# Attention weights of first halves turned by TensorE instead of by transfer, in a two-layer decoder trunk

## The chip, the cores and the metric

The kernel runs on one core of one Trainium2 chip. The metric is device time in microseconds (us) of one execution. The kernel before takes 1116.9 us, the median of three runs from 1115.07 to 1117.86.

## The reference

Two pre-norm residual layers work on 1024 positions of width 1024, and a last RMSNorm closes. Layer 0 is an RG-LRU: an input product, a causal convolution, two block-diagonal gates, a linear recurrence, an output product. Layer 1 is attention with a forget gate, 16 heads of 64. Cut to what matters here:

```python
u = h @ w_in                       # q, k, v, gate, f_logit
cum = cumsum(log_sigmoid(f_logit + b_f))
logits = einsum("bqhd,bkhd->bhqk", q, k) / 8
logits = logits + cum_q[..., None] - cum_k[:, None]
logits = where(kpos <= qpos, logits, -1e30)
o = einsum("bhqk,bkhd->bqhd", softmax(logits), v)
x = x + (o * silu(gate)) @ w_out
return rms_norm(x, final_g)
```

All inputs and outputs are float32.

## The kernel before

TensorE does nearly all products three times, in a format of its own for float32 (hi x hi, hi x lo, lo x hi), where hi is a rounded copy (`to_hi`, a cast) and lo the rest (`to_lo`, a subtraction). Layer 0 fills the first 447 us or so and the change doesn't touch it. Attention runs from about 484 us on, head by head, and is what this document is about.

**A head.** The 1024 queries of a head are two halves `c` of 512, and each half has four rows `i` of 128 queries. Row `i` sees keys 0 to (i+1) x 128. `maxima(hd, c)` makes the rows of one half, from the longest down: TensorE multiplies into a PSUM tile `S`; DVE adds the mask and finds the maximum (L773); ACT takes exp (L778) into a tile `p` (or `pp`, a tile that holds two rows). After the rows of the second half the sums are turned into factors: their transpose goes to `rc`, by DMA to `recd`, and comes back as `recb`, spread over partitions (`fetch_sums`). `weigh(hd, c)` then multiplies the weights with the values into `O`. For that the weights must stand with keys on the partitions, so they have to be turned. There are two ways:

- by TensorE: 128x128 transposes (L61) into a PSUM tile `pt`, out of which ACT writes `ph` (hi) and DVE `pl` (lo). `pt` has two slots in PSUM and shares them with `S`, so every tile of the one kind waits for the slot that an earlier one of either kind leaves;
- by transfer (`by_dma`): for the two longest rows of a half, DVE turns 32x32 blocks (`turn_row`, L733), one DMA writes them to DRAM (`turnd`, L738 or L740), and four DMAs read them back into `pp` in the order wanted (L745). `ph` and `pl` are then read from `pp`. The remaining blocks of that half go through TensorE.

**Sections.** Head `hd` has two sections. The first runs `weigh(hd, 0)` beside `maxima(hd, 1)`: rows 7, 6, 5, 4 of S. The second runs `weigh(hd, 1)` beside `maxima(hd + 1, 0)`: rows 3, 2, 1, 0 of the next head. Each is driven by a string, where `1` is the next step of `maxima`, `0` the next step of `weigh`, and `.` one fill step: six 128x512 matmuls, about 1.39 us of TensorE, of the projections of later heads (`kq_units`, `g_units`) or, in the last heads, of the output product. The strings are `ORDER` for heads 0 to 11 and `LAST` for heads 12 to 15. A `side` generator gives one step per fill step: stores of y, sums, scaling, weights.

**The other parts that the change touches.** `scale(hd)` multiplies the gate `sg` by `recb` on GpSimd (POOL), and `gated(hd, c)` multiplies `yo` by it, also on POOL; `put_away` splits y and stores it; `settle` calls `fetch_sums`, `scale` and `gated(hd, 0)` in the second section. After heads 3, 7 and 11 come the values of the next four heads: `value_weights` loads and splits their weights in the second section, and `values` makes 192 matmuls of 128x256 (tile `vps`). `late` loads and splits, in head 14, the part of the output weights that is used last (L1092); its raw tiles `wf` come from the same ring of three buffers as those of `split_out` (L108), which feed the output product that fills TensorE at that time. SP's queue issues all DMAs, one after the other.

Of the kernel before, what the change touches and what calls it, by code (L numbers as in the profile page):

```python
# [11 lines left out]
F32 = mybir.dt.float32  # L12
# [5 lines left out]
P = 128  # L18
SEQ = 1024
HALF = 512  # L20
# [3 lines left out]
HD = 64  # L24
EPS = 1e-6
GROUP = 2
ORDER = "1.0.1.10.1..0", "10.1.0.10.1.0.0"
LAST = "1..0.1..10..1..0", "10..1.0..10..1.0..0"
NEG = -1e30
PSUM = bass.MemoryType.PSUM  # L30
# [8 lines left out]
def trunk(ctx: ExitStack, tc: tile.TileContext, xt, w0, wg, wo0, pc, gn, gf, w1, wv, wf, bf, wo1, out):  # L39
# [11 lines left out]
    wpool = ctx.enter_context(pool("w", 4))  # L51
# [450 lines left out]
    with ExitStack() as l1:  # L502
# [24 lines left out]
        def value_weights(g, parts):  # L527

            waiting = []
            for k in range(0, KT + 2, 2):  # L530
                if k < KT:
                    wt = wpool.tile([P, 2, 256], F32, tag="wf", name="wf", bufs=3)
                    nc.sync.dma_start(wt, wv[g, :, k : k + 2])
                    waiting.append(wt)
                if k:
                    own = wpool if k <= 4 else vwpool
                    hi = own.tile([P, 2, 256], F32R, tag="wh", name="wh")
                    lo = own.tile([P, 2, 256], F32R, tag="wl", name="wl")
                    with tc.issue_after(seen[0].ins):
                        to_hi(hi, waiting[0], nc.scalar)  # L540
                    with tc.issue_after(masked[0].ins):
                        to_lo(lo, waiting.pop(0), hi, nc.vector)
                    parts += [(hi[:, i], lo[:, i]) for i in range(2)]
                yield

        def values(g, parts):

# [171 lines left out]
            return two_rows[c][:, r * size : r * size + n]  # L719

        def by_dma(hd, c):
            return 0 < 2 * hd + c < 27

        written, turns = [None], {}

# [82 lines left out]
        def scale(hd, cs=slice(0, SEQ)):  # L808
            rows = slice((hd % 2) * HD, (hd % 2 + 1) * HD)
            for b in range(cs.start, cs.stop, HALF):  # L810
                part = slice(b, b + HALF)
                sg = sgs[hd // 2][rows, part]
                nc.gpsimd.tensor_tensor(sg, sg, recs[hd // 2][rows, part], ALU.mult)  # L813
# [93 lines left out]
        def gated(hd, c, sub=slice(0, HALF)):  # L907

            if hd % 2 == 0:
                return  # L910
            pair = hd // 2
            yo = yos[pair, c][:, sub]
            nc.gpsimd.tensor_tensor(
                yo, yo, sgs[pair][:, c * HALF + sub.start : c * HALF + sub.stop], ALU.mult
            )
            if hd == 15:
                split_y(c, pair, yo, sub)

        def put_away(hd, c):
            if hd % 2 == 0 or hd > 12:  # L920
                return
            pair = hd // 2
            yo = yos[pair, c]
            yh = at.tile([P, HALF], F32R, tag="xp", name="yh", bufs=2)
            with tc.issue_after(seen[0].ins):
                to_hi(yh, yo, nc.scalar)
            with tc.issue_after(masked[0].ins):
                to_lo(yo.bitcast(F32R), yo, yh, nc.vector)
            for part, y in enumerate((f32(yh), yo)):
                nc.sync.dma_start(y1d[c, pair, part], y)  # L930

        def settle(hd):
            yield
            yield
            with tc.issue_after(written[0].ins):
                fetch_sums(hd)
            yield
            scale(hd)
            gated(hd, 0)

        def put_later(hd):
            for c in range(2):
                yield
                yield
                put_away(hd, c)

        def beside(*gens):
            for _ in itertools.zip_longest(*gens):
                yield
# [135 lines left out]
        def late():  # L1085

            for half in range(2):
                wh, wl = (kqpool.tile([P, 8, P], F32R, tag=f"qk{p}{half}", name=f"wo{p}") for p in "hl")
                for b in range(2):
                    wt = wpool.tile([P, 4, P], F32, tag="wf", name="wf", bufs=3)  # L1090
                    for d in range(2):
                        nc.sync.dma_start(wt[:, 2 * d : 2 * d + 2], wo1[half * 4 + b * 2 + d, :, 6:8])  # L1092
                    sl = slice(4 * b, 4 * b + 4)

                    with tc.issue_after(seen[0].ins):
                        to_hi(wh[:, sl], wt, nc.scalar)
                    to_lo(wl[:, sl], wt, wh[:, sl], nc.vector)
                    yield
                late_w.append((wh, wl))
# [16 lines left out]
        for hd in range(HEADS):  # L1116
# [18 lines left out]
            elif pair < 6:  # L1135
                fill = chain(kq_units(pair + 1, ((0, (1,)),)), late_q(hd + 1), g_units(pair + 1))
            first, second = LAST if hd > 11 else ORDER
            side = put_later(hd - 1) if hd else iter(())
            run(first, weigh(hd, 0), maxima(hd, 1), fill=fill, side=side)
            drain(side)  # L1140
            if hd == HEADS - 1:
# [4 lines left out]
                scale(hd)  # L1146
            side = late() if hd == 14 else settle(hd)
            if hd % 4 == 3 and hd < 12:

                parts = []  # L1150
                side = beside(side, value_weights(hd // 4 + 1, parts))
            run(second, weigh(hd, 1), maxima(hd + 1, 0), fill=fill, side=side)
            drain(side)
            gated(hd, 1)
            if hd == 13:
                with tc.issue_after(seen[0].ins):
                    split_y(0, 6, yos[6, 0])
# [90 lines left out]
```

## Time and profile before

| | |
|---|---|
| median of three runs | 1116.9 us |
| lowest and highest | 1115.07 and 1117.86 us |
| profiled execution | 1114.79 us |
| its span | 1113.0 us |
| mean granted TensorE clock | 0.995 |
| TensorE busy | 1088.5 us of the span |

The span goes from the first to the last instruction of the profiled execution; the 1.8 us between it and the execution's own time lie around the program. The profiled execution is 2.1 us shorter than the median. "Busy" is the time in which an engine executes; a TensorE matmul's end is modelled, so its idle times are read from the start of one matmul to the start of the next. A row of the timeline gives start, duration, engine, line, operation and tile; in brackets stands the idle time before it and who ended it. In the windows view a row has the stretch, its length, the busy time of PE (matmuls), PEld (weight loads), DVE, ACT and POOL with their instructions, the granted clock (1.00 is full), the share of the DMA engines and GB/s.

### The profile page before, as it was taken

To read this page: it belongs to the slowest core of one execution; us is meant where nothing else is said; L and a number is where in the kernel's file an instruction comes from. 1 tells how busy PE (TensorE), PEld (TensorE's weight loads), DVE (VectorE), ACT (ScalarE), POOL (GpSimd) and SP (SyncE) were. 2 spreads that over 40 slices of the span, in tenths; PEclk is the share of its full clock that TensorE was granted. 3 is DMA by queue.
4 is the path that set the end of the run, shared out by engine and by line. 5 is a ranking of instruction groups with operands and counts; after the bars stand their busy time and mean duration, and the time that the engine had idled before them with its cause. 6 is when DMAs were issued, how large, how long until landed. Compare 5 with 4: busy or idle time off the path is not lost.

```text
span 1113.0 us, 15892 instructions
## 1 busy us (share of the span) xinstructions
PE 1088.5 (98%) x5645; PEld 921.1 (83%) x5645; DVE 792.1 (71%) x1280; ACT 579.9 (52%) x1037; POOL 171.8 (15%) x120
## 2 busy tenths in 40 slices
PE   9999999999999999999999999999999999998997
PEld 7787888888888888987888888788888898887886
DVE  8888755876569787757887478874788757666445
ACT  8487345355454665545555355553556535434335
POOL 2312212111121201420121101111012110110010
PEclk9999999999999999999999999999999999999999
DMA  6111111111112113445767357674477845785344
GB/s 220 62 53 42 52 53 48 48 54 45 43 48 71 48 65 116 130 124 162 199 192 195 118 161 193 200 198 123 150 189 213 198 126 166 248 266 174 109 147 189
DMA packets 100919, 145.81 MB, mean 131 GB/s; under 512 B 25348, under 2 KB 53636, under 8 KB 100840
## 3 DMA queue, kind: packets, MB, share of 16 engines
q1 hardware_dynamic: 100840, 144.80, 43.6%
q8 instruction: 44, 0.72, 0.3%
q14 instruction: 35, 0.29, 0.1%
HBM read 83.48 MB, written 36.11 MB: 107 GB/s over the span
## 4 chain that ended last, share of the span: by engine, by line
PE 76%; DVE 7%; DMA 6%; issue 5%; ACT 4%; SPq 1%; POOL 1%; ACTq 0%; DVEq 0%; POOLq 0%
PE gps L57 26%; PE ops L57 16%; PE ups L57 10%; PE vps L57 7%; PE S L57 5%; PE O L57 4%; PE gate L57 3%; PE turn L57 2%; PE pt L61 2%; DVE pl L98 2%; ACT pp L778 1%; DMA T<-qkl 1%; DVE S L773 1%; DMA U<-qkh 1%; DMA turnd<-turn 1%
## 5 line engine op out<-in xcount | busy, mean ns | idle before, releaser
L57 PE MATMUL gps<-hh,wh 128*128 128x512 f32 x576 | 229.4, 398 | 0.0
L57 PE MATMUL gps<-hh,wl 128*128 128x512 f32 x576 | 225.6, 392 | 0.2 <-POOL wl L98 0.2
L57 PE MATMUL gps<-hl,wh 128*128 128x512 f32 x576 | 225.1, 391 | 0.0
L87 ACT CAST wh<-wf 128x512 fp32r<-128x512 f32 (+2 forms) x156 | 94.2, 607 | 138.0 <-PE ops L57 43.1
L98 POOL TENSOR_TENSOR wl<-wf,wh 128x512 fp32r<-128x512 f32 (+1 forms) x60 | 99.5, 1664 | 378.1 <-ACT wh L87 260.3
L57 PEld LDWEIGHTS gps<-hl,wh 128*128 128x128 f32 x576 | 108.2, 188 | 23.6
L57 PEld LDWEIGHTS gps<-hh,wl 128*128 128x128 f32 x576 | 108.7, 189 | 18.7 <-POOL wl L98 0.6
L57 PEld LDWEIGHTS gps<-hh,wh 128*128 128x128 f32 x576 | 108.5, 188 | 18.5
L813 POOL TENSOR_TENSOR sg<-sg,recb 64x512 f32<-64x512 f32 x32 | 44.4, 1407 | 487.6 <-DMA recb<-recd 445.7
L773 DVE CUSTOM_DVE_ANT_0 S<-S,mask 128x512 f32<-128x512 f32 (+7 forms) x128 | 97.0, 758 | 24.7 <-PE S L57 24.4
L778 ACT ACTIVATE pp<-S,m 128x512 f32<-128x512 f32 (+1 forms) x64 | 54.4, 851 | 87.9 <-DVE m L773 87.8
L57 PE MATMUL S<-T,U 128*128 128x512 f32 (+7 forms) x384 | 92.6, 350 | 4.0 <-ACT pp L778 4.0
L98 DVE TENSOR_TENSOR wl<-wf,wh 128x512 fp32r<-128x512 f32 x96 | 68.6, 720 | 22.6 <-ACT wh L87 22.5
L57 PEld LDWEIGHTS S<-T,U 128*128 128x128 f32 (+1 forms) x384 | 67.5, 190 | 20.8 <-ACT pp L778 9.1
L375 DVE TENSOR_TENSOR x<-x,ops 128x512 f32<-128x512 f32 x80 | 54.1, 680 | 41.2 <-PE ops L57 41.2
L57 PE MATMUL O<-pl,v 128*128 128x256 f32 (+3 forms) x302 | 77.2, 290 | 2.2 <-DMA T<-qkl 1.2
L57 PE MATMUL O<-ph,v 128*128 128x256 f32 (+3 forms) x302 | 78.8, 289 | 0.0
L57 PE MATMUL ups<-hh,wl 128*128 128x512 f32 x192 | 75.3, 392 | 0.8 <-POOL wl L98 0.8
L57 PE MATMUL ups<-hh,wh 128*128 128x512 f32 x192 | 75.7, 395 | 0.0
L57 PE MATMUL ups<-hl,wh 128*128 128x512 f32 x192 | 75.2, 392 | 0.2 <-DVE hl L232 0.2
L57 PE MATMUL vps<-wh,hh 128*128 128x256 f32 (+1 forms) x256 | 73.3, 287 | 2.0 <-DVE v L575 1.0
L57 PE MATMUL ops<-yh,wh 128*128 128x512 f32 x192 | 75.2, 392 | 0.0
(170 smaller groups left out, 2372.3 us busy)
## 6 DMA issues: line engine op xcount, KB each, us to landing
wf<-in_w SPq DMA_DIRECT2D x100, 256.0 KB
turnd<-turn SPq DMA_DIRECT2D x26, 448.0 KB
pp<-turnd SPq DMA_DIRECT2D x52, 224.0 KB
wf<-in_wo SPq DMA_DIRECT2D x64, 128.0 KB
U<-qkh SPq DMA_DIRECT2D x64, 128.0 KB
T<-qkh SPq DMA_DIRECT2D x28, 256.0 KB
turnd<-turn SPq DMA_DIRECT2D x13, 384.0 KB
pp<-turnd SPq DMA_DIRECT2D x52, 96.0 KB
```

What stands on the lines that cost most here:

```text
L57: pe[0] = nc.tensor.matmul(*args, **kw)
L61: pe[0] = nc.tensor.transpose(*args)
L87: nc.scalar.copy(hi, src)
L98: return eng.tensor_tensor(lo, src, f32(hi), ALU.subtract)
L375: nc.vector.tensor_tensor(x, x, pt, ALU.add)
L773: masked[0] = nc.vector.tensor_tensor_reduce(S[:, :n], S[:, :n], mask[:, SEQ - n :], -1.0, -NEG, ALU.add, ALU.min, accum_out=m)
L778: seen[0] = nc.scalar.activation(p, S[:, :n], AF.Exp, bias=m, scale=-1.0, accum_out=sums[:, i : i + 1])
L813: nc.gpsimd.tensor_tensor(sg, sg, recs[hd // 2][rows, part], ALU.mult)
```

## The change

First halves of heads 1 to 13, whose two longest rows went by transfer, are now turned by TensorE as a whole; second halves of heads 0 to 12 stay with the transfer. Each such head has ten transposes in its first section where it had four (seven in a first `pt` tile, three in a second), and eight O matmuls of 512, 384, 256 and 128 columns where it had twelve of 256 and 128. Per head, two DVE turns of 384 columns, one write to DRAM and four reads go. The strings in `ORDER` place the fill steps otherwise. `scale` and `gated` of heads up to 11 are emitted with the first fill step of the next head (before: `scale` and `gated` of the first half with the third fill step of the second section, and `gated` of the second half behind that section), and the stores of y one fill step later. The value weights' first pieces are loaded and split in the first section of heads 3, 7 and 11, and their buffers come from the two pools the other way round. The first of each two raw tiles in `late` takes the buffer of `turn` instead of one of the ring.

```diff
-ORDER = "1.0.1.10.1..0", "10.1.0.10.1.0.0"
+ORDER = "1.0..1.10.1.0", "10..1.0.10.10.0"
...
-                    own = wpool if k <= 4 else vwpool
+                    own = vwpool if k <= 4 else wpool
...
                 yield
+                if k < 4:
+                    yield
...
         def by_dma(hd, c):
-            return 0 < 2 * hd + c < 27
+            return c == 1 and hd < 13
...
-        def put_away(hd, c):
-            if hd % 2 == 0 or hd > 12:
+        def store_y(hd, c):
+            if hd % 2 == 0:
                 return
...
             with tc.issue_after(written[0].ins):
                 fetch_sums(hd)
-            yield
+            if hd > 11:
+                yield
+                scale(hd)
+                gated(hd, 0)
+
+        def put_away(hd):
             scale(hd)
-            gated(hd, 0)
-
-        def put_later(hd):
             for c in range(2):
-                yield
-                yield
-                put_away(hd, c)
+                gated(hd, c)
+            for c in range(2):
+                yield
+                yield
+                yield
+                store_y(hd, c)
...
                 for b in range(2):
-                    wt = wpool.tile([P, 4, P], F32, tag="wf", name="wf", bufs=3)
+                    if b:
+                        wt = wpool.tile([P, 4, P], F32, tag="wf", name="wf", bufs=3)
+                    else:
+                        wt = at.tile([P, 7 * P], F32, tag="turn", name="wf", bufs=1)[:, :HALF]
+                        wt = wt.rearrange("p (d j) -> p d j", j=P)
...
             first, second = LAST if hd > 11 else ORDER
-            side = put_later(hd - 1) if hd else iter(())
+            side = put_away(hd - 1) if 0 < hd < 13 else iter(())
+            if hd % 4 == 3 and hd < 12:
+                parts = []
+                coming = value_weights(hd // 4 + 1, parts)
+                side = beside(side, itertools.islice(coming, 5))
             run(first, weigh(hd, 0), maxima(hd, 1), fill=fill, side=side)
...
             if hd % 4 == 3 and hd < 12:
-
-                parts = []
-                side = beside(side, value_weights(hd // 4 + 1, parts))
+                side = beside(side, coming)
             run(second, weigh(hd, 1), maxima(hd + 1, 0), fill=fill, side=side)
             drain(side)
-            gated(hd, 1)
+            if hd > 11:
+                gated(hd, 1)
```

The order on TensorE in the first section of head 3, from row 5 of S on. Before (`T`, `U` are keys and queries, `v_...` the values of one block of keys):

```order
L57 MATMUL S<-T_3593,U_3596 128x512 x2
L57 MATMUL S<-T_3593,U_3596 128x256 x2
L57 MATMUL O<-ph,v_3757 128x256
L57 MATMUL O<-pl,v_3757 128x256
L57 MATMUL O<-ph,v_3789 128x128
L57 MATMUL O<-pl,v_3789 128x128
```

The same place in the changed kernel:

```order
L57 MATMUL S<-T_3593,U_3596 128x512 x2
L57 MATMUL S<-T_3593,U_3596 128x256 x2
L61 MATMUL pt<-ident,pp 128x128 x3
L57 MATMUL O<-ph,v_3757 128x512
L57 MATMUL O<-pl,v_3757 128x512
L57 MATMUL O<-ph,v_3789 128x384
L57 MATMUL O<-pl,v_3789 128x384
```

Three transposes into a second `pt` tile now stand right behind row 5, and the products behind them are wider.

On TensorE, the end of the second section that comes before it, from row 0 of S on (`gps_5100` is the fill step's tile). Before:

```order
L57 MATMUL S<-T_3593,U 128x256 x2
L57 MATMUL gps_5100<-hh,wh 128x512
L57 MATMUL gps_5100<-hh,wl 128x512
L57 MATMUL gps_5100<-hl,wh 128x512
L57 MATMUL gps_5100<-hh,wh 128x512
L57 MATMUL gps_5100<-hh,wl 128x512
L57 MATMUL gps_5100<-hl,wh 128x512
L57 MATMUL O<-ph,v_3757 128x256
L57 MATMUL O<-pl,v_3757 128x256
```

And in the changed kernel:

```order
L57 MATMUL S<-T_3593,U 128x256 x2
L57 MATMUL O<-ph,v_3757 128x256
L57 MATMUL O<-pl,v_3757 128x256
L57 MATMUL O<-ph,v_4007 128x128
L57 MATMUL O<-pl,v_4007 128x128
```

The fill step between row 0 and the products of the half turned by transfer is gone from here; it stands two steps further up, ahead of row 2.

On SP's queue, the loads of output weights in head 14 (L1092 is `late`, L108 is `split_out`; `x1d`, `xp` are the running sums of the output product; `recd`, `recb` the softmax sums of the head). Before:

```order
L1092 DMA wf<-in_wo 128x256 x2
L1006 DMA xp<-x1d 128x512
L1010 DMA x1d<-xp 128x512
L794 DMA recd<-rc 8x128
L1006 DMA xp<-x1d 128x512
L803 DMA recb<-recd 64x1024
L1092 DMA wf<-in_wo 128x256 x2
L108 DMA wf<-in_wo 128x512
L108 DMA wf<-in_wo 128x256
```

And in the changed kernel, where `late` stands on L1103:

```order
L1103 DMA wf<-in_wo 128x256 x2
L1017 DMA x1d<-xp 128x512
L108 DMA wf<-in_wo 128x512
L1013 DMA xp<-x1d 128x512
L108 DMA wf<-in_wo 128x256
L1017 DMA x1d<-xp 128x512
L796 DMA recd<-rc 8x128
L1013 DMA xp<-x1d 128x512
L805 DMA recb<-recd 64x1024
L1103 DMA wf<-in_wo 128x256 x2
```

The two loads of `split_out` that came behind the last late tile now stand ahead of the sums of head 14 and of that tile.

## The prediction

> **What bounds the kernel now.** First the page's head and its busy line, to see which engine carries the span.
>
> ```profile
> span 1113.0 us, 15892 instructions
> PE 1088.5 (98%) x5645; PEld 921.1 (83%) x5645; DVE 792.1 (71%) x1280; ACT 579.9 (52%) x1037; POOL 171.8 (15%) x120
> ```
>
> TensorE (PE) is busy for 98% of the span: 24.5 us of it are idle, so no change that leaves TensorE's work alone can bring more than that plus what a lowered clock costs. Next the windows view, cut into the stage before attention, the heads 0 to 13 and the end (columns: length, then busy time and instructions of PE, weight loads, DVE, ACT, POOL, then granted clock, DMA share, GB/s).
>
> ```profile
> 0.00:484.00 484.00, 481.26 (x2218) 400.54 (x2219) 358.27 (x442) 272.46 (x360) 102.92 (x70) 1.00 0.22 71
> 484.00:912.00 428.00, 416.66 (x2406) 358.79 (x2405) 319.12 (x611) 221.03 (x484) 52.97 (x38) 1.00 0.64 176
> 912.00:1113.00 201.00, 190.54 (x1025) 161.81 (x1023) 114.73 (x227) 86.36 (x194) 15.95 (x13) 0.97 0.54 180
> ```
>
> The change doesn't touch the first stage. In the other two TensorE idles for 11.3 and 10.5 us. So I cut attention into each head's two sections, at the first matmul of row 7 and of row 3 of S: nine first sections that show what a first section costs, then the nine second sections that carry no values (three of them and the sum), then the three that carry values (one of them, and the sum).
>
> ```profile
> 502.16:517.58 15.42, 14.19 (x71) 11.50 (x70) 12.06 (x21) 7.92 (x16) 0.00 (x0) 1.00 0.42 146
> 561.03:575.06 14.03, 13.48 (x70) 11.19 (x69) 12.96 (x22) 8.58 (x17) 3.75 (x3) 1.00 0.50 173
> 591.04:604.24 13.20, 13.20 (x70) 11.19 (x69) 10.64 (x20) 7.15 (x14) 0.00 (x0) 1.00 0.49 141
> 700.87:715.41 14.54, 13.47 (x70) 11.18 (x69) 13.50 (x22) 8.82 (x18) 4.28 (x4) 1.00 0.56 185
> 841.60:855.03 13.43, 13.43 (x70) 11.20 (x69) 12.50 (x22) 8.82 (x18) 4.97 (x4) 1.00 0.57 193
> ```
>
> ```profile
> 575.06:591.04 15.98, 14.90 (x88) 12.56 (x86) 12.72 (x26) 7.62 (x19) 2.97 (x2) 1.00 0.91 234
> 686.35:700.87 14.52, 14.52 (x87) 12.44 (x86) 10.54 (x23) 7.99 (x19) 1.14 (x1) 1.00 0.86 232
> 827.09:841.60 14.51, 14.51 (x88) 12.43 (x86) 10.55 (x23) 8.11 (x19) 1.01 (x1) 1.00 0.92 238
> sum 137.96, PE 133.44 PEld 112.73 DVE 106.99 ACT 69.66 POOL 20.26; mean PE 14.83 PEld 12.53 DVE 11.89 ACT 7.74 POOL 2.25
> ```
>
> ```profile
> 604.24:644.12 39.88, 38.58 (x280) 35.77 (x278) 22.23 (x46) 17.32 (x41) 5.43 (x4) 1.00 0.49 128
> sum 119.95, PE 115.98 PEld 107.31 DVE 65.80 ACT 51.85 POOL 16.42; mean PE 38.66 PEld 35.77 DVE 21.93 ACT 17.28 POOL 5.47
> ```
>
> A first section without a wait takes 13.20, a second one 14.51. What lies above these floors is loss. Second sections lose 137.96 - 9 x 14.51 = 7.4 together, and the ones that lose most are those in which POOL is busy for nearly 3 us within the section.
>
> **Part 1, the work that TensorE takes over.** Heads 1 to 13 get six more transposes each. The chain of waits prices one:
>
> ```profile
> 1016.89 0.88 PE pt L61 x8
> ```
>
> 0.88 / 8 = 0.11, so 0.66 a head. The products of the first half stream the same 2,560 columns in 8 matmuls instead of 12; four starts fewer give a little back. I take 0.55 (bounds 0.5 and 0.66). None of it can hide, since TensorE is the engine that is full: 13 x 0.55 = **+7.2** (6.5 to 8.6). What goes on the other side is work of DVE and of the queues:
>
> ```profile
> L733 DVE STREAM_TRANSPOSE turn<-pp 128x384 f32<-128x384 f32 x26 | 14.9, 571 | 3.2 <-ACT pp L778 3.2
> ```
>
> 26 stream transposes of 571 ns, and per head one write of 384 KB and four reads of 96 KB. DVE works 12.9 us in a second section of 16 and has slack, so these 14.9 us are worth nothing by themselves; they count only where a wait below ends on DVE or a transfer.
>
> **Part 2, first sections.** Head 0's first half is turned by TensorE already, so its section shows what heads 1 to 11 get. It takes 15.42: 0.55 of extra work, and 1.67 of waits, nearly all at one place (timeline, head 0; in brackets the idle time before and its releaser).
>
> ```profile
> 506.86 1.08 PE L57 MATMUL S<-T,U 128*128 128x512 f32 x4
> 507.88 1.12 DVE L98 TENSOR_TENSOR pl<-pt,ph 128x512 fp32r<-128x512 f32 x2
> 508.91 1.09 DVE L773 CUSTOM_DVE_ANT_0 S<-S,mask 128x896 f32<-128x896 f32 x1
> 509.16 0.92 PE L57 MATMUL S<-T,U 128*128 128x512 f32 x4
> 511.24 0.55 PE L61 MATMUL pt<-ident,pp 128*128 128x128 f32 x3 [1.17 <-ACT pp L778]
> ```
>
> The three late transposes need the PSUM slot of row 6 of S, which is free only when row 6 has been masked and its exp is done. Their start was due at about 509.86 (the pair of S matmuls at 509.16 issues in 0.70) and came at 511.24, 1.38 late. The mask began at 508.91 and not at 507.94, where S ended, since the pl of the first transposes stood ahead of it on DVE. The new string puts one fill step more between those transposes and S, so pl will be done in time and 0.97 of the 1.38 goes; 0.41 stays, because one fill step and a row of S still lie between row 6 and the transposes. This new wait comes in each of 12 heads: 4.9. Beside it the sections of heads 2, 6 and 10, which now lose 0.83, 1.34 and 0.23 with POOL at work beside them, keep an estimated 0.4 each: 1.2. Before, the twelve lost 1.67 + 0.83 + 1.34 + 0.23 = 4.1 (the others nothing). So 6.1 - 4.1 = **+2.0** (bounds -4.1, no wait left, and 12 x 1.38 + 1.2 - 4.1 = +13.7, head 0's whole wait in every head).
>
> **Part 3, second sections.** The string now leaves no fill step between row 0 of S and the products O of the half that was turned by transfer. The timeline of head 2, first one wait and two issues of SP's queue:
>
> ```profile
> 578.46 0.62 PE L57 MATMUL S<-T,U 128*128 128x384 f32 x2 [0.39 <-ACT pp L778]
> ...
> 583.38 0.55 SPq L621 DMA_DIRECT2D T<-qkh  x1
> 583.98 0.59 SPq L622 DMA_DIRECT2D T<-qkh  x1
> ```
>
> The same timeline by its compute engines, from row 1 of S to the section's end:
>
> ```profile
> 583.09 0.40 PE L57 MATMUL S<-T,U 128*128 128x256 f32 x2
> 585.16 0.69 DVE L98 TENSOR_TENSOR pl<-pp,ph 128x512 fp32r<-128x512 f32 x1 [1.14 <-ACT ph L87]
> 585.18 0.40 PE L57 MATMUL S<-T,U 128*128 128x256 f32 x2
> 585.98 0.69 DVE L98 TENSOR_TENSOR pl<-pp,ph 128x512 fp32r<-128x512 f32 x1
> 586.81 0.28 PE L57 MATMUL O<-ph,v 128*128 128x256 f32 x1
> 587.50 2.97 POOL L813 TENSOR_TENSOR sg<-sg,recb 64x512 f32<-64x512 f32 x2 [22.64 <-DMA recb<-recd]
> 588.01 2.75 DVE L98 TENSOR_TENSOR pl<-pp,ph 128x512 fp32r<-128x512 f32 x2 [1.34 <-ACT ph L87]
> 590.81 0.39 PE L57 MATMUL O<-pl,v 128*128 128x256 f32 x1 [0.68 <-DVE pl L98]
> ```
>
> With the fill step gone, O would start right behind the S of 585.18, at 585.4, where it now starts at 586.81. The first pl is ready at 585.85 and the second at 586.67; counted through the products between, O waits 0.4 for the first and 0.2 more for the second: **0.6 in each of nine heads**, 5.4. In return there is a fill step more between the eight transposes and row 2 of S, so the wait there (0.39, at 578.46) goes.
>
> The end wait is another matter. POOL's scale starts when recb has landed, at 587.50, and the two pl behind it take 2.75 where one of 512 columns takes 0.69; O then waits 0.68. In the even heads the fetch of recb moves behind the two loads of T on SP's queue that now follow it (0.55 and 0.59 to issue, plus their transfer), and away from the write that stood ahead of it. An estimate is 1.7 later, at 589.2. The pl begin an estimated 0.4 later than now, at 588.4, and take 1.2 without POOL: an overlap of 0.4, which at half the pace costs 0.4, half of which the products feel. So 9 x (0.6 + 0.2) = 7.2 against 7.4 now: **-0.2** (bounds -7.4, no wait left, and +8, rival two).
>
> The Trainium skill, SBUF — State Buffer, section "Who interferes with whom", says that the port pair which VectorE and GpSimd share is an exclusive lock, held for a whole instruction by whichever started first. By that rule, a pl that has begun before POOL loses nothing, so the term would be 9 x 0.2 = 1.8 lower and the sum 1.8 lower as well; the 2.75 above, about one POOL instruction (2.97 / 2) more than the pl alone, agrees with it.
>
> **Part 4, values.** A second section with values would take 14.51 plus 192 vps matmuls, 144 of which the chain of waits shows as one unbroken piece:
>
> ```profile
> 626.77 17.51 PE vps L57 x144
> ```
>
> 17.51 / 144 = 0.1216, so 14.51 + 23.35 = 37.86; three make 113.6 against 119.95, a loss of 6.4. It lies in the part where vps is scattered among the O's while its weights are still being split. Now the weights are begun one section earlier and vps comes as two whole pieces around row 1 and row 0 of S, which give the masks, the exps and the pl room: I leave 1.4 of the 6.4: **-5.0** (bounds -6.4 and -1.5).
>
> **Part 5, late weights.** In head 14 TensorE stands still, and what follows runs slowly (timeline; chain of waits; windows of PE alone, clock first after the busy time).
>
> ```profile
> 1028.72 0.79 PE L57 MATMUL ops<-yhh,wh 128*128 128x512 f32 x1 [3.15 <-ACT wh L87]
> 1029.98 0.79 PE L57 MATMUL ops<-yhh,wl 128*128 128x512 f32 x1 [0.47 <-DVE wl L98]
> ```
>
> ```profile
> 1023.49 3.90 DMA wf<-in_wo
> ```
>
> ```profile
> 1028.70:1034.60 5.90, 5.41 (x16) 0.50 0.50 172
> ```
>
> The wait for the weights is 3.15 + 0.47, and the granted clock is 0.50 for the next 5.90, which costs half of that, 2.95: 6.6 in all. The Trainium skill, TensorE: Matmul & The Clock Gate, Part 1, says that an idle window of about 3.4 us halves the rate; this trace agrees, with 3.15 idle and then 0.50. The weights are late because their transfers stand on SP's queue behind a late weight tile that waits for a buffer of the same ring. With two of the four late tiles in another buffer, the order shows them ahead. I leave 0.6: **-6.0** (bounds -6.6 and 0).
>
> The stores of y, the gating and the swapped pools I cost at nothing: POOL has 85% idle, the stores move one fill step, and SP waits for none of them longer than for the loads around. If the stores held SP's queue up, recb would come later still, which part 3 wants rather than fears.
>
> **Sum.** 7.2 + 2.0 - 0.2 - 5.0 - 6.0 = -2.0. The profiled execution took 1114.8 (span 1113.0), so 1112.8 for one like it. The median of the runs before is 1116.9, 2.1 above the profiled one; set against the median the forecast is **1114.9**.
>
> **Rivals.** One, faster: POOL's scale always lands behind the last pl, the first sections' new wait is absorbed by DVE's freed 14.9 us, values and late weights give all they lose. Parts 2 to 5 then give 0, -2.0, -6.4 and -6.6, with +7.2 together -7.8: 1109.1. For it: 686.35 and 827.09 above show sections at their floor; against it: the 0.41 and the 0.6 are worked out from chains that the freed time doesn't shorten. Two, slower: the scale lands among the pl in every head, instead of behind them. Row 0 of S and the pl move later, by the fill step ahead of them less the waits that go; if recb lands less than about 1 later than now, one pl is held for a whole scale instruction, 1.5, of which O's slack takes 0.4: 1.1 a head, 9 x (1.1 - 0.2) = +8.1, 1123.0. For it: head 2's rows show just that now; against it: SP's queue puts recb behind T. Three, slower: the late weights come no sooner, since two late tiles still take a place in the ring, and the clock falls again: part 5 is 0, 1120.9. Four, slower: the two PSUM slots become the bound of first sections. Twelve tiles instead of eleven pass through them in each head, and if the mask of row 6 stays late for another reason than the pl of head 0, the whole 1.38 stays in twelve heads: part 2 at +13.7, 1126.6. For it: head 0 has this wait; against it: the added fill step.
>
> Rival five is a matter of the clock. Head 0's section holds ten transposes and its granted clock is 1.00, so six more a head should leave it there; if each head fell to 0.50 once for 5.9, as after the wait in head 14, twelve heads would cost 12 x 2.95 = 35: 1150. The Trainium skill, TensorE: Matmul & The Clock Gate, Part 4, says that transposes don't count as busy time of the kind that raises the clock; the 1.00 of head 0 speaks against its mattering here.
>
> **How the numbers follow.** A measurement of this kernel can tell about 0.3%, 3.4 us, from no change. Chances: the forecast 0.42, rival one 0.29, two 0.14, three 0.08, four 0.05, five 0.02. The forecast's own spread, some 4 us either way, lies mostly within 0.3% (1113.5 to 1120.3) and reaches the faster side; it gives 0.12 to faster, 0.27 to the same and 0.03 to slower. Rival one gives 0.27 to faster and 0.02 to the same; rivals two to five give 0.05 to the same and 0.24 to slower. Faster 0.39, same 0.34, slower 0.27. The range takes in rivals one and two with some of their bounds: 1106 to 1124.
>
> **What would show it.** Right: first sections of heads 1 to 11 at about 14.2, with 0.4 of waits ahead of the three late transposes; second sections near 15.3, with a wait on pl right behind row 0 of S and little at the end; value sections near 38.3; no idle stretch of 3 us in head 14 and a clock of 1.00 there. Wrong: first sections above 15, a wait at the end of every second section with POOL at work beside it, or the clock still at 0.50 after head 14's weights.

## The result, and the profile after

The changed kernel takes 1124.07 us, the median of six runs from 1121.06 to 1125.88, against 1116.66 for six runs of the kernel before. The ratio is 1.0065, with a 95% interval from 1.0047 to 1.0082: slower, by about 7 us, where 1114.9 was forecast. The profiled execution took 1123.92 with a span of 1122.1, 9.1 more than the span before. The medians differ by 7.4 only, since the profiled execution of the kernel before lay 2.1 below its median; the parts below are parts of the two spans.

The page's head and the three stages, cut at about the same places of the program (912 before and 924 here both lie within head 11's section with values, not behind head 13, as the prediction has it):

```profile
span 1122.1 us, 15840 instructions
PE 1096.1 (98%) x5671; PEld 927.7 (83%) x5671; DVE 789.2 (70%) x1254; ACT 580.2 (52%) x1037; POOL 176.5 (16%) x120
```

```profile
0.00:484.00 484.00, 481.07 (x2217) 399.70 (x2218) 357.70 (x442) 272.43 (x360) 101.91 (x70) 1.00 0.22 71
484.00:924.00 440.00, 423.87 (x2409) 364.85 (x2408) 317.36 (x586) 220.53 (x482) 57.71 (x38) 1.00 0.54 150
924.00:1122.10 198.10, 191.20 (x1049) 163.18 (x1047) 114.19 (x226) 87.23 (x195) 16.86 (x13) 1.00 0.55 179
```

The middle stage grew and the last one shrank. The DMA share of the middle went from 0.64 to 0.54: the transfers did go, and it bought no time there. The first sections of heads 0, 2, 3 and 6, and the sum of heads 0 to 11:

```profile
502.29:516.48 14.19, 13.89 (x71) 11.67 (x70) 11.66 (x19) 7.36 (x14) 0.00 (x0) 1.00 0.37 139
561.31:575.74 14.43, 13.91 (x72) 11.68 (x71) 13.03 (x20) 7.32 (x15) 5.75 (x4) 1.00 0.37 135
592.41:606.59 14.18, 13.88 (x73) 11.67 (x71) 11.73 (x20) 7.91 (x15) 0.00 (x0) 1.00 0.51 147
705.81:720.50 14.69, 13.90 (x72) 11.67 (x71) 12.95 (x20) 7.32 (x15) 4.19 (x4) 1.00 0.30 119
...
sum 171.42, PE 166.58 PEld 140.07 DVE 144.72 ACT 90.66 POOL 14.14; mean PE 13.88 PEld 11.67 DVE 12.06 ACT 7.55 POOL 1.18
```

All are now between 14.16 and 14.7, where before the same twelve sum to 162.99. The second sections without values (heads 0, 1, 2 and the sum of nine), then those with values:

```profile
516.48:532.22 15.74, 14.98 (x87) 12.70 (x87) 11.58 (x24) 8.47 (x21) 3.23 (x2) 1.00 0.69 160
546.39:561.31 14.92, 14.72 (x87) 12.65 (x87) 9.90 (x23) 8.52 (x21) 0.24 (x1) 1.00 0.88 211
575.74:592.41 16.67, 15.56 (x88) 12.71 (x88) 12.70 (x25) 8.78 (x22) 3.00 (x2) 1.00 0.73 183
...
sum 142.14, PE 135.66 PEld 114.36 DVE 103.39 ACT 78.15 POOL 21.63; mean PE 15.07 PEld 12.71 DVE 11.49 ACT 8.68 POOL 2.40
```

```profile
606.59:646.79 40.20, 38.62 (x279) 35.88 (x279) 20.42 (x42) 16.30 (x40) 6.89 (x4) 1.00 0.39 100
...
sum 121.57, PE 116.76 PEld 108.73 DVE 61.57 ACT 48.94 POOL 20.04; mean PE 38.92 PEld 36.24 DVE 20.52 ACT 16.31 POOL 6.68
```

Again the sections with POOL at work for 3 us (15.74, 16.67) stand above the one without (14.92). Last, the second section of head 14, 27.92 before:

```profile
1031.71:1052.99 21.28, 21.28 (x114) 17.90 (x114) 14.71 (x31) 10.47 (x24) 2.54 (x2) 1.00 0.54 167
```

No idle time, and a clock of 1.00. The difference of 9.1 by parts, beside what was forecast for each:

| part | forecast | changed kernel |
|---|---|---|
| first sections of heads 0 to 13: more work, and waits | +9.2 | 171.42 - 162.99, and 0.49 + 0.48 in heads 12 and 13: +9.4 |
| nine second sections without values | -0.2 | 142.14 - 137.96: +4.2 |
| three with values | -5.0 | 121.57 - 119.95: +1.6 |
| head 14, late weights | -6.0 | 21.28 - 27.92: -6.6 |
| all else | 0 | +0.5 |
| sum | -2.0 | +9.1 |

The first and the fourth part came near their forecasts. The loss stands in the two kinds of second sections. The timeline of head 2's second section shows how:

```profile
583.66 0.47 SPq L805 DMA_DIRECT2D recb<-recd  x1
...
587.41 0.69 DVE L98 TENSOR_TENSOR pl<-pp,ph 128x512 fp32r<-128x512 f32 x1 [1.14 <-ACT ph L87]
587.75 0.40 PE L57 MATMUL S<-T,U 128*128 128x256 f32 x2
587.93 3.00 POOL L815 TENSOR_TENSOR sg<-sg,recb 64x512 f32<-64x512 f32 x2 [20.79 <-DMA recb<-recd]
...
588.40 3.08 DVE L98 TENSOR_TENSOR pl<-pp,ph 128x512 fp32r<-128x512 f32 x2
...
589.85 0.39 PE L57 MATMUL O<-pl,v 128*128 128x256 f32 x1 [0.73 <-DVE pl L98]
```

recb is fetched 7.9 us into the section (583.66 after 575.74; before it was 7.7), and POOL's scale, which waits for it, starts 4.3 later, at 587.93, just ahead of the second pl. That pl and the next take 3.08 together, where the first took 0.69. O waits 0.73 for them. Something else is late in this head, and in heads 6 and 10 too: ACT stands for a weight tile, and row 2's exp stands behind that cast.

```profile
583.48 0.62 ACT L87 CAST wh<-wf 128x512 fp32r<-128x512 f32 x1 [1.48 <-DMA wf<-in_w]
584.01 0.57 ACT L780 ACTIVATE pp<-S,m 128x384 f32<-128x384 f32 x1
```

In head 0 the first pl behind row 0 is waited for by itself, and POOL then holds the last ones:

```profile
528.06 0.39 PE L57 MATMUL O<-pl,v 128*128 128x256 f32 x1 [0.20 <-DVE pl L98]
528.43 3.23 POOL L815 TENSOR_TENSOR sg<-sg,recb 64x512 f32<-64x512 f32 x2 [41.71 <-DMA recb<-recd]
529.30 2.64 DVE L98 TENSOR_TENSOR pl<-pp,ph 128x512 fp32r<-128x512 f32 x2 [0.49 <-ACT ph L87]
532.00 0.39 PE L57 MATMUL O<-pl,v 128*128 128x256 f32 x1 [0.55 <-DVE pl L98]
```

And in head 3, with values, POOL's scale and the gating behind it (L915) run from the first pl to the last:

```profile
620.71 3.47 POOL L815 TENSOR_TENSOR sg<-sg,recb 64x512 f32<-64x512 f32 x2 [29.78 <-DMA recb<-recd]
621.41 0.38 PE L57 MATMUL O<-pl,v 128*128 128x256 f32 x1 [0.34 <-DVE pl L98]
621.48 1.55 DVE L98 TENSOR_TENSOR pl<-pp,ph 128x512 fp32r<-128x512 f32 x1
623.09 0.39 PE L57 MATMUL O<-pl,v 128*128 128x256 f32 x1 [0.71 <-DVE pl L98]
623.22 2.94 DVE L98 TENSOR_TENSOR pl<-pp,ph 128x512 fp32r<-128x512 f32 x2
624.26 1.62 POOL L915 TENSOR_TENSOR yo<-yo,sg 128x512 f32<-128x512 f32 x1
626.22 0.38 PE L57 MATMUL O<-pl,v 128*128 128x256 f32 x1 [0.53 <-DVE pl L98]
```

So two theories stood for the loss: POOL's scale among the pl (rival two, and the same in the heads with values), or the missing fill step behind row 0, where O would wait for exp, ph and pl whatever POOL does. The experiments part them, and price the other parts one by one. Every ratio below is to the kernel before, on the same chip. Differences in us between two kernels are of medians, which were partly taken on different chips; by the ratios they come out up to 3 us otherwise.

### The profile page after: what moved, and what is told of

It is laid out like the page before. It is cut to its first block, busy times and chain, and to the rows that moved or that the text cites. A ratio compares the mean times of both kernels' runs of the same rounds, so it can differ in the third digit from the quotient of the medians.

```text
span 1122.1 us, 15840 instructions
## 1 busy us (share of the span) xinstructions
PE 1096.1 (98%) x5671; PEld 927.7 (83%) x5671; DVE 789.2 (70%) x1254; ACT 580.2 (52%) x1037; POOL 176.5 (16%) x120
## 4 chain that ended last, share of the span: by engine, by line
PE 72%; DVE 8%; DMA 7%; issue 6%; ACT 4%; SPq 2%; POOL 1%; ACTq 0%; DVEq 0%; POOLq 0%
PE gps L57 23%; PE ops L57 16%; PE ups L57 10%; PE vps L57 8%; PE S L57 4%; PE O L57 3%; DMA wf<-in_w 3%; PE gate L57 2%; PE turn L57 2%; DVE pl L98 2%; PE pt L61 2%; DVE S L775 2%; DMA turnd<-turn 1%; ACT pp L780 1%; ACT ph L87 1%
## 5 line engine op out<-in xcount | busy, mean ns | idle before, releaser
L815 POOL TENSOR_TENSOR sg<-sg,recb 64x512 f32<-64x512 f32 x32 | 48.0, 1518 | 499.5 <-DMA recb<-recd 499.5
L98 DVE TENSOR_TENSOR pl<-pt,ph 128x512 fp32r<-128x512 f32 (+1 forms) x108 | 65.3, 633 | 26.3 <-ACT ph L87 26.2
```

Source lines behind the costliest of these rows:

```text
L98: return eng.tensor_tensor(lo, src, f32(hi), ALU.subtract)
```

## The experiments

**Late weights alone.** The kernel before with the new buffers in `late`:

```diff
-                    wt = wpool.tile([P, 4, P], F32, tag="wf", name="wf", bufs=3)
+                    if b:
+                        wt = wpool.tile([P, 4, P], F32, tag="wf", name="wf", bufs=3)
+                    else:
+                        wt = at.tile([P, 7 * P], F32, tag="turn", name="wf", bufs=1)[:, :HALF]
+                        wt = wt.rearrange("p (d j) -> p d j", j=P)
```

> The kernel before with the late weights' buffers of the change and nothing else. Theory (the late weights are the part of the change that works, and works by itself): head 14's second section falls from 27.9 us to about 21.3, the idle 3.15 us and the clock of 0.50 go, and the whole gets 6.6 us shorter, to about 1110. Rival (the weights come in time only because the turn buffer and the transfers of first halves are out of the way): less than 2 us.

1110.49, ratio 0.9938 (0.9923 to 0.9954). Head 14's second section:

```profile
1017.95:1039.23 21.28, 21.28 (x114) 17.90 (x114) 14.94 (x31) 10.58 (x24) 2.52 (x2) 1.00 0.55 168
```

The same 21.28 as in the changed kernel. This part is worth its 6.6 us alone, and the turning of first halves has nothing to do with it.

**A later fetch, first try.** The changed kernel; in `settle`, for even heads and heads 3, 7 and 11:

```diff
-            yield
-            yield
+            for _ in range(9 if hd < 12 and (hd % 2 == 0 or hd % 4 == 3) else 2):
+                yield
```

> The changed kernel, with the fetch of the sums (recb) put at the end of the second section in heads with an even number and in heads 3, 7 and 11, so that POOL's scale starts in the next first section or beside the last values. Theory (POOL's scale among the pl costs the second sections their time): the waits of 0.7 to 1.0 us on pl go in six even heads and two of them in each head with values, 6 x 0.8 + 3 x 1.5 = 9 us shorter, to about 1115. Rival (O waits for the chain of exp, ph and pl behind row 0 by itself, whatever POOL does): less than 2 us.

1124.61, ratio 1.0065 (1.0049 to 1.0081), as the changed kernel. It tells nothing on either theory, since the edit did not move the fetch: in the timeline of head 2, recb is still fetched at 585.00, 8.3 into the section, behind the same two loads of T, and POOL's scale runs from 588.68. Here the place of emission didn't set this DMA's place in SP's queue; something that it must wait for did, in the tied fetch below.

**A fill step behind row 6.** The changed kernel with another first string:

```diff
-ORDER = "1.0..1.10.1.0", "10..1.0.10.10.0"
+ORDER = "1.0.1..10.1.0", "10..1.0.10.10.0"
```

> The changed kernel with the second fill step of the first section moved from ahead of row 6 of S to behind it. Theory (the three late transposes wait 0.41 us for the slot of row 6, whose mask and exp take 2.5 us): the wait goes in twelve heads, 12 x 0.41 = 4.9 us shorter, to about 1119. Rival (row 6's mask is then late behind the pl of the first transposes, as in head 0 of the kernel before): the two cancel, within 1.5 us of 1124.

1131.27, ratio 1.0117 (1.0094 to 1.0139): slower than the changed kernel by 7 us, against both theories. The first sections sum to 176.12, 4.7 more; in head 0 the wait ahead of the three late transposes is gone, but row 6 itself now comes 0.3 late and row 4 is 0.6 late:

```profile
515.09 0.87 PE L57 MATMUL S<-T,U 128*128 128x320 f32 x4 [0.43 <-ACT p L780]
```

So the wait of 0.41 is no lone gap to be filled: with the fill step moved, other tiles of the two PSUM slots wait, and longer. The rest of the loss is in the heads with values (129.08 for the three), where the granted clock fell to 0.92, 0.96 and 0.92 of full (more on this in the last section).

**First halves by transfer again.** The changed kernel with

```diff
-            return c == 1 and hd < 13
+            return 0 < 2 * hd + c < 27
```

> The changed kernel with the first halves of heads 1 to 13 turned by transfer again, everything else as changed. Theory (TensorE's own work of 0.55 us in thirteen heads and the wait of 0.41 ahead of the three late transposes in eleven cost what they were reckoned at, and DVE and the queues gain nothing that TensorE feels): 7.2 + 4.5 = 11.7 us shorter, to about 1112. Rival (the transfers that come back delay recb, the pl or the fill weights by as much): no gain beyond 4 us.

1113.26, ratio 0.9953 (0.9933 to 0.9972), and a span 10.6 shorter than the changed kernel's. The sum came as expected, but not where. First sections fall from 171.42 to 167.78 and those of heads 12 and 13 by 1.0, 4.6 in all instead of 11.7, since the changed string doesn't suit the transfers (14.1 where the old string took 13.2). The rest comes from second sections (137.40) and those with values (119.19). Head 0's timeline shows why: its pl take 0.69 again, because the fetch waits in SP's queue behind the third load of T and the write that came back (L742).

```profile
524.93 1.20 SPq L742 DMA_DIRECT2D turnd<-turn  x1
526.22 1.24 SPq L805 DMA_DIRECT2D recb<-recd  x1
...
532.08 2.54 POOL L815 TENSOR_TENSOR sg<-sg,recb 64x512 f32<-64x512 f32 x2 [44.90 <-DMA recb<-recd]
```

The scale now starts at 532.08, at the section's end, instead of 528.43 in the middle of the pl. In all six even heads it starts 14.5 to 15.2 us into the section, where the changed kernel has 12.0 to 12.6.

**A later fetch, tied.** The changed kernel, with recb's fetch made to wait for the end of the second section (in the heads named above; the steps of the first try stay, and the issue is also put behind the last instruction of TensorE):

```diff
+            if held:
+                rows = slice(s * HD, (s + 1) * HD)
+                nc.vector.tensor_copy(recs[pair][rows, :1], yos[pair, 1][rows, :1])
             nc.sync.dma_start(
```

> The changed kernel, with the fetch of recb tied to the end of the second section in even heads and in heads 3, 7 and 11: one element of yo, which is ready there, is copied into recb's tile ahead of the transfer that overwrites it. Theory (POOL's scale among the pl): the scale now starts over 4 us behind the section, every pl takes 0.7 us or less, the waits of 0.7 to 1.0 on pl go, 8 us shorter, about 1116; what stays in second sections is 0.4 to 0.6 right behind row 0. Rival (O's wait comes from the chain of exp, ph and pl, whatever POOL does): less than 2 us.

1112.85, ratio 0.9978 (0.9968 to 0.9987), 11 us shorter than the changed kernel. Its timeline for head 2, and the sums of the nine second sections and of the three with values:

```profile
587.26 0.69 DVE L98 TENSOR_TENSOR pl<-pp,ph 128x512 fp32r<-128x512 f32 x1 [1.14 <-ACT ph L87]
588.26 0.69 DVE L98 TENSOR_TENSOR pl<-pp,ph 128x512 fp32r<-128x512 f32 x1
589.44 1.03 DVE L98 TENSOR_TENSOR pl<-pp,ph 128x512 fp32r<-128x512 f32 x2 [0.49 <-ACT ph L87]
```

```profile
sum 137.83, PE 134.83 PEld 114.09 DVE 94.51 ACT 78.17 POOL 1.39; mean PE 14.98 PEld 12.68 DVE 10.50 ACT 8.69 POOL 0.15
```

```profile
sum 115.22, PE 113.95 PEld 107.31 DVE 54.32 ACT 48.65 POOL 15.27; mean PE 37.98 PEld 35.77 DVE 18.11 ACT 16.22 POOL 5.09
```

In the nine sections POOL is now busy for 1.39 us instead of 21.63, and the pl of head 2 take 0.69 where two of them took 3.08. 142.14 became 137.83 and 121.57 became 115.22: 10.7 of the span's 11.5. The theory of POOL's scale holds, and without this collision both missing terms come to what the prediction had: -0.1 and -4.7, against -0.2 and -5.0. The edit also lets the loads behind the fetch move up in SP's queue, which was not tested by itself.

**The same in the kernel before.** Late weights alone, and the tied fetch in even heads:

```diff
-            yield
-            yield
-            with tc.issue_after(written[0].ins):
-                fetch_sums(hd)
+            held = hd < 12 and hd % 2 == 0
+            for _ in range(9 if held else 2):
+                yield
+            with tc.issue_after((pe if held else written)[0].ins):
+                fetch_sums(hd, held=held)
```

> The kernel before with the late weights' buffers of the change, and the fetch of recb tied to the section's end in even heads in the same way. Theory: the six even heads without values, 15.3 to 16.4 us in the kernel with the late weights alone, fall by the 0.7 to 1.4 us that pl loses to POOL, to 14.9, 5.5 us together: about 1105. Rival (later fetches stand in the way of the loads behind them on SP's queue, or POOL's scale then holds up the masks of the next first section): no gain, about 1110.

1107.61, ratio 0.9930 (0.9915 to 0.9945), against 0.9938 for late weights alone: no difference of the whole that can be told, where 5.5 us were expected. By the two profiled executions (spans 1108.5 and 1105.3) it is 3 us shorter. The nine second sections fall from 138.32 to 133.66, 4.7, and the heads with values, which were left as they were, came out 2.1 longer (122.50 against 120.36). What was expected of the even heads happened, at 15.01 to 15.06 each.

**Value weights as before.** The changed kernel without its edits to `value_weights` and to the place where it starts:

> The changed kernel with the value weights loaded and split as before (in the second section only, buffers from the same pools as before). Theory (the early weights put vps ahead of row 1, so that the transferred half's pl fall where POOL's scale runs, and the three heads with values lose what they should have gained): three sections of 40.2 to 41.1 come down to 39.7 or so, 2 to 3 us shorter. Rival (early weights do take 5 us off the waits of vps and hide behind the waits of O): three sections 41.5 to 42, 4 us longer.

1123.19, ratio 1.0067 (1.0051 to 1.0084): no difference that can be told from the changed kernel, and both theories missed. The heads with values take 123.81, 2.2 more, as the rival said in direction; but the second sections of heads 2, 6 and 10, now at 15.78 each like the other even heads, give 2.5 back (139.62). The early weights gain in the one and lose in the other.

**The old string behind row 0.** The changed kernel with

```diff
-ORDER = "1.0..1.10.1.0", "10..1.0.10.10.0"
+ORDER = "1.0..1.10.1.0", "10.1.0.10.1.0.0"
```

> The changed kernel with the string of the second section as before, so that a fill step stands between row 0 of S and O again. Theory (0.4 to 0.6 us of wait on the first pl come from the missing fill step): this wait goes in twelve heads, 6 us, and 0.4 comes back ahead of row 2 in six: 3 to 4 us shorter, if POOL's scale meets the pl as before; about 1120. Rival (POOL's scale alone costs the second sections their time): within 2 us of 1124.

1115.92, ratio 1.0010 (0.9994 to 1.0026), 8 us shorter than the changed kernel, twice what was expected. Its profiled execution, at 1119.76, was one of the longest of its runs, and there the nine sections (142.20) have gained nothing, because POOL's scale now meets the pl of odd heads as well (16.08 in head 5); the three with values gained 3.6 (117.95). How the other 4 us come about in its shorter runs was not seen.

**Both.** The changed kernel with the tied fetch and the old second string:

> The changed kernel with recb's fetch tied to the section's end, and the second section's string as before. Theory (two separate losses: POOL's scale, 8 us or more, and the missing fill step behind row 0, about 0.45 in twelve heads): second sections without values go from 137.8 to about 134.5 together, the whole to about 1109; what stays against the kernel best1 is TensorE's own work and the waits ahead of the three late transposes, 7 or 8 us in first sections. Rival (the wait ahead of row 2 comes back in all heads and eats it): no change, about 1113.

1108.92, ratio 0.9918 (0.9894 to 0.9942), 4 us shorter than the tied fetch alone, as expected, but otherwise shared out: the nine sections fell by 1.3 to 136.57 and the three with values by 2.2 to 113.01. The missing fill step is a loss of its own, on balance about 0.3 in each of twelve heads, beside POOL's; head 5, where POOL's scale now meets the pl, lost 0.75 (15.70 against 14.95).

**The gains without the turning.** The kernel before with late weights, the early value weights and their pools, and the tied fetch in even heads and in heads 3, 7 and 11:

> The kernel before (first halves turned by transfer, strings as before) with the late weights' buffers, the early value weights and their pools of the change, and the fetch of recb tied to the section's end in even heads and in heads 3, 7 and 11. Theory (the change's gains, late weights 6.6 and values 4 to 5, are independent of who turns the first halves, and POOL was what hid the second one): sections with values 115 to 117 together, against 122.5 in the kernel with late weights and even heads' fetch alone, 2 or 3 us lost in second sections of heads 2, 6 and 10 to the early splits: about 1104. Rival (the early value weights only move the wait, as in the changed kernel, where taking them out changed the time by under 1 us): about 1108.

1107.12, ratio 0.9907 (0.9877 to 0.9937): the shortest median of the study, though not to be told from 1107.61. In the heads with values TensorE is now busy throughout, 112.66 (the prediction's floor for them was 113.6), and yet the time is no better than expected by the rival, since heads 2, 6 and 10 lose what they win: 16.52, 17.10 and 18.72. The timeline of head 10:

```profile
858.85 0.62 ACT L87 CAST wh<-wf 128x512 fp32r<-128x512 f32 x1 [4.64 <-DMA wf<-in_w]
859.37 0.57 ACT L780 ACTIVATE pp<-S,m 128x384 f32<-128x384 f32 x1
```

ACT stood 4.64 us for a weight tile, and row 2's exp stood behind that cast in its queue.

**The pools.** The same kernel with

```diff
-                    own = vwpool if k <= 4 else wpool
+                    own = wpool if k <= 4 else vwpool
```

> The kernel best1 with the pools of the value weights not exchanged. Theory (the exchange of pools lets a cast of gate weights move ahead of row 2's exp on ACT in heads 2, 6 and 10, and this cast waits for its transfer): these three second sections, 16.5, 17.1 and 18.7 in best1, come back to 15.0, 7 us shorter, about 1100, with values still near 113. Rival (the early start of the value weights does it, by the places it takes in the ring of raw tiles): no change in heads 2, 6 and 10, within 2 us of 1107.

1108.77, ratio 0.9918 (0.9900 to 0.9936). Heads 2, 6 and 10 are back at 14.5, so the exchange of pools is what set that cast's place, but the 7 us did not come, since the wait only moved: the first sections of heads 3, 7 and 11 now take 16.87, 15.31 and 15.63 and the values 116.95. The time is the same.

**Turning by TensorE, all else equal.** The shortest kernel with first halves turned by TensorE and both strings as before (`by_dma` as in the change):

> The kernel best1 with first halves turned by TensorE and both strings as before. Theory (TensorE's own 0.55 in thirteen heads, and, with the string as before, head 0's waits of 1.4 to 1.7 ahead of the three late transposes in all heads): first sections 15.2 to 15.6, 20 to 25 us more together than in best1, about 1128. Rival (head 0's wait is its own; DVE's freed 0.57 us a row lets the mask of row 6 come in time): first sections of 14.2 as in the changed kernel, about 1115.

1120.39, ratio 1.0026 (1.0015 to 1.0037), 13 us longer than with transfers. First sections sum to 181.68, 16.2 more, between the two expectations: 14.8 to 15.1 in most heads and 15.5 to 16.1 in heads 0, 2, 6 and 10. The first of head 1's late transposes:

```profile
541.20 0.55 PE L61 MATMUL pt<-ident,pp 128*128 128x128 f32 x3 [0.92 <-ACT pp L780]
```

In head 0 of the changed kernel this idle time is 0.30 (the row is shown below). The changed kernel's first string, with its fill step ahead of row 6, is thus worth some 11 us over the twelve heads, 181.68 against 170.46 in the kernel with the tied fetch and the old second string, which differ in the stores of y as well.

## Why the prediction was wrong

**First sections** came out right as a sum, and the row that was foreseen is there in head 0, at 0.51 of idle time for the weight load and 0.30 for the matmul:

```profile
511.48 0.55 PE L61 MATMUL pt<-ident,pp 128*128 128x128 f32 x3 [0.30 <-ACT pp L780]
```

14.2 was forecast and 14.16 to 14.20 measured, 14.43 to 14.69 in the sections with POOL at work. Rival four is out: 1.38 did not stay. Within the sum two errors offset each other, which is luck. Heads 12 and 13 show the work alone, since TensorE waits nowhere in their first sections: 0.49 and 0.48, not 0.55. That makes about 6.2 of work in thirteen heads, for 7.2, and leaves 3.2 of the 9.4 for the waits, for 2.0.

**Late weights** were right, and shown by themselves.

**Second sections** failed at two steps. The first is "An estimate is 1.7 later, at 589.2". It said that recb would land later because its fetch would stand behind two loads of T. The order was as stated; the time was not. The fetch in head 2 before:

```profile
582.80 0.48 SPq L803 DMA_DIRECT2D recb<-recd  x1
```

The two loads that stand ahead of it in the changed kernel (its fetch, at 583.66, is shown above):

```profile
582.03 0.51 SPq L623 DMA_DIRECT2D T<-qkh  x1
582.59 0.59 SPq L624 DMA_DIRECT2D T<-qkh  x1
```

The loads of T were issued earlier as well (582.03 in head 2, 6.3 into the section, where before they stood at 8.3), and the write of 384 KB that had stood ahead of the fetch was gone. So the fetch was issued where it was before, 7.1 to 8.5 us into the section in even heads, and POOL's scale started at 12.0 to 12.6. In the run with first halves by transfer again, and so with the write back, the scale did come late enough, at 14.5 to 15.2: turning these halves by TensorE took away a delay of the size that the prediction counted on. The last two pl hardly moved either, from 12.95 to 12.8 into the section in heads 0, 4 and 8, so the collision stayed. These two take 2.63 or 2.64 there and 1.03 in heads 1, 5 and 9, where POOL is out of the way, and the section takes 15.74 against 14.92: 0.82 lost, where 0.2 was forecast. The tied fetch won 4.3 of it back over the nine sections.

This was rival two in its mechanism, which was given 0.14. Its condition (recb less than about 1 us later than now) was the right one to ask for, and the evidence set against it, the place in the queue, was no evidence of a time. That its 1123.0 lies near the 1124.07 is luck: it put +7.9 on the nine second sections, where +4.2 came, and it left out the heads with values, which came out 6.6 above their forecast.

The second step is that "the swapped pools" were costed at nothing. The early value weights with their swapped pools cost heads 2, 6 and 10 some 2.5 us, since they let a cast of gate weights stand ahead of an exp on ACT.

The other half of this term, the wait behind row 0, was right in kind: in odd heads the first pl starts 0.49 after the ph ahead of it, where 0.12 is the spacing, 0.37 late; 0.6 was forecast. That the tied fetch brings the second sections to -0.1 is thus partly chance: the loss to the casts took the place of end waits of 0.2 and of a part of the 0.6, which were reckoned and did not come.

**Values** failed at a step that was left out: POOL's scale has no place in that term. In head 3, before, the pl lay at 10 and at 17 us into the section, and the scale at 12.7 (12.3 to 13.3 in the three heads), between the two. In the changed kernel the fill step ahead of row 2 and sixteen vps ahead of row 1 push the pl to 14 us and more, where the scale starts too, at 14.1 to 14.7. The 1.4 of waits that the prediction left were the waits of vps only. With the scale moved away, the three heads gain 4.7 of the 5.0.

TensorE's own work and the waits in first sections (9.2 together) were thus priced right, and the change was a loss but for the late weights: everything else together is +15.7. With the tied fetch the rest is still a loss, by the ratios 0.9978 and 0.9938 (late weights alone).

One reading in the prediction is off, and nothing rests on it: DVE works 12.72 us in the second section that it shows, not 12.9.

## What to carry to other kernels

A place in a queue is not a time: before a collision is taken to go or to come, work out when the operations ahead become ready, and where both partners then lie. Count what leaves a queue as well as what joins it. When two engines slow each other, tie the one that nobody waits for to an event behind the other; in the changed kernel that was worth 10 or 11 us and needed one copied element, while in the kernel before it won 4.7 us in its sections and nothing of the whole that can be told. And price the parts of a mixed change one by one: the one edit of buffers was worth 6.6 us, and the rest took it back twice over.

## What the runs showed of the hardware

DVE's pl and POOL's scale slow each other. In head 3 a pl of 0.69 took 1.55, and two of them 2.94, while POOL's instructions grew as well: 3.47 for two that take 2.52 when alone (the scale at 532.08 above took 2.54). The pl that was under way when POOL began, at 587.41 in head 2, kept its 0.69. The Trainium skill, SBUF — State Buffer, section "Who interferes with whom", gives the cause as a port pair that one of the two engines holds alone for a whole instruction, and these numbers agree with it, though no row shows the port itself.

The granted clock fell without a long idle stretch. In head 11's section with values, TensorE was busy for 2.14 of 3.60 us in a row of short waits on ph and pl, none of them over 0.72 by itself, and then:

```profile
910.00:913.60 3.60, 2.14 (x12) 0.93 0.65 186
913.60:917.20 3.60, 3.60 (x15) 0.60 0.01 2
```

Fill matmuls were spaced 0.43 us instead of 0.23 there. In head 3 of the run with the fill step behind row 6 it was 1.98 busy of 4.00 us, and then 0.50 for the next 5.80. So a cluster of waits can cost once more behind itself, but need not: heads 3 and 7 of the changed kernel, with 2.55 and 2.35 busy of 3.60, stayed at 1.00. The Trainium skill, TensorE: Matmul & The Clock Gate, Part 1, speaks of an idle window of about 3.4 us, and further on of short idle times between groups of matmuls; here it took no such window. Nor did it take all of the 3.15 us in head 14 of the kernel before, which the prediction sets beside that window: the last matmul started at 1025.18, and the granted clock was 0.80 from 1027.50 to 1028.00 and 0.50 from there on.

Transposes did not lower the clock: the first section of head 0 with its ten shows 1.00, as all the others that now have ten.
